# Feature-major rotary queries and key in an MLA layer, with the parts placed by DMAs

## The chip, the cores and the metric

One core of one Trainium2 chip runs the whole program. The metric is the device time of one execution in microseconds; the time of a kernel is the median of its runs. The engines are called by their short names: PE (TensorE, matmuls), ACT (ScalarE), DVE (VectorE), POOL (GpSimd) and SP (SyncE, which here only issues DMAs). A name such as SPq stands for the queue that an engine issues from.

## The reference

A trunk of two layers over 512 tokens of width 1024. Layer 0 is multi-head latent attention (MLA), layer 1 is gated linear attention (GLA); each is followed by a squared-ReLU MLP, and a final RMSNorm ends it. Only the MLA mixer is changed here:

```python
def mla_mixer(xn, positions, w_in, q_norm, w_uq, kv_norm, w_ukv, w_o):
    h = xn @ w_in                                  # 1024 -> 384 + 256 + 64
    c_q, c_kv, k_rope = h[..., :384], h[..., 384:640], h[..., 640:]
    q  = (rms_norm(c_q,  q_norm)  @ w_uq ).reshape(B, S, 8, 128 + 64)
    kv = (rms_norm(c_kv, kv_norm) @ w_ukv).reshape(B, S, 8, 128 + 128)
    q_nope, q_rope = q[..., :128], q[..., 128:]
    k_nope, v      = kv[..., :128], kv[..., 128:]
    cos, sin = rope_tables(positions)              # 32 frequencies
    q_rope = apply_rope(q_rope, cos, sin)          # (t1 cos - t2 sin, t2 cos + t1 sin)
    k_rope = apply_rope(k_rope, cos, sin)          # one rotary key for all heads
    # scores = (q_nope . k_nope + q_rope . k_rope) * 192**-0.5, causal softmax, times v, times w_o
```

All inputs and outputs are float32.

## The kernel before

Precision comes from splitting: a float32 operand becomes a rounded part `hi` and a rest `lo`, both in the matmul's fp32r format, and `mm3` multiplies them in three matmuls (L107 to L112). `split` makes `hi` on ACT and `lo` on DVE. Activations are kept feature-major, that is features in the 128 partitions and the 512 tokens along the free axis.

The order of instructions on each engine is made by a scheduler when the program is built: it goes by the order of the text and by its own estimate of when each operand is ready. Each engine then works its list strictly in order and waits on semaphores. `tc.issue_after` and `keep_in_program_order` put instructions behind others in that order. SP's queue is also such a list: a DMA that waits holds back those behind it. Tiles come from pools with a fixed number of buffers: raw weights (`wraw`) have two, the `hi` and `lo` weights (`wh`, `wl`) three each, scratch (`tmp`) six, and `slot("B")` sixteen. The accumulators (PSUM banks) have three tags: "a" with two banks, "b" and "c" with three each.

The MLA function goes through these steps:

- The latents: `pkv` (two banks, L402 to L409) and the three query latents `CQ`. `latent` (L382) makes their parts and sums their squares. Neither latent is normalised before it is used: the 1/rms of each token is applied later.
- The raw rotary key (L440 to L450): weights with `lo` in 64 columns and `hi` in 64, 16 matmuls, and a copy `kr` of all 128 rows.
- The means (L453 to L459): eight matmuls with stationary tiles 96 wide, three rows of 32 equal lines, for the latent keys, the queries and x. `rsqrt` (Ln and Exp on ACT, then three steps on DVE) turns them into `rows`.
- V (L462 to L513): 8 blocks of 6 matmuls. After the third block `rows` is turned into columns `cols` by four transposes, and `evac_v` copies V out, scaled by a column. Row 0 is split and spread over 128 partitions by two matmuls (L505) into `r_kv`, which scales the latent keys `CKV`.
- The rotary tables: `rope_turns` (L293) works out the angles in turns on POOL from `gains`, with tokens in the partitions and (4 tiles x 32 frequencies) along the free axis. `rope_tables` (L346) takes the Sin after the V blocks, between two table loads of ACT, and scales one copy of the tables for the queries and one by x's 1/rms for the key.
- The key is turned token-major by four transposes (L519), rotated, and turned back by four (L611); `KA` and `KB` hold its parts in opposite halves.
- The rotary queries (L528 to L543): 36 matmuls, token-major, four tiles. `rotate_q(t, g)` (L626) rotates a tile of four heads, part of it on POOL for the second group. `turn_q` (L637) turns two heads back by four transposes and makes their parts.
- `project(h)` (L547) makes the other 128 features of q and k; `scores`, `turn` and `values` are the attention proper, and project the heads two ahead.

At the start the loads go out on SP's queue and two of x on ACT's (L1397 to L1408), and `exp_set` loads ACT's table for Ln and Exp.

Of the kernel before, what the change touches and what calls it, by code (L numbers as in the profile page):

```python
# [18 lines left out]
P = 128  # L19
D = 1024  # L20
# [18 lines left out]
SCALE = (NOPE + ROPE) ** -0.5  # L39
# [9 lines left out]
def trunk_kernel(ctx: ExitStack, tc: tile.TileContext, t_in: dict, out: bass.AP, out_row: bass.AP):  # L49
# [98 lines left out]
    gains = const.tile([P, N_GAIN + NT + 32], F32, name="gains")  # L148
    pos_i = gains[:, N_GAIN : N_GAIN + NT].bitcast(I32)
    invf = gains[:, N_GAIN + NT :]  # L150
# [33 lines left out]
    row_eps = rk.tile([3 * RB, 1], F32, name="row_eps")  # L184
    DVE.memset(row_eps[: 2 * RB], EPS * EPS)
    DVE.memset(row_eps[2 * RB :], EPS)

    def row_weights(name, *parts):
        t = rk.tile([P, 3 * RB], F32, name=name)
        DVE.memset(t, 0.0)  # L190
        for lo, hi, v in parts:
            DVE.memset(t[:, lo * RB : hi * RB], v)
        both = tuple(rk.tile([P, 3 * RB], F32R, name=name + x) for x in "hl")
        split(t, *both, hi_eng=DVE)
        return both

    mean_kv = row_weights("mean_kv", (0, 1, 1.0 / KL))
    mean_q = row_weights("mean_q", (1, 2, 1.0 / QL))
    mean_x = row_weights("mean_x", (0, 2, EPS / D), (2, 3, 1.0 / D))

# [4 lines left out]
    def rsqrt(r, m, n, eps=eps_t):  # L205
# [9 lines left out]
        DVE.scalar_tensor_tensor(r, b, 1.5, y0, ALU.add, ALU.mult)  # L215
# [77 lines left out]
    def rope_turns():  # L293
        sh = (P, NT, 32)
# [3 lines left out]
        def tmp(shape, dt=F32):  # L298
            return rp.tile(list(shape), dt, tag="rope", bufs=8, name=uname("rope"))

        pos = tmp((P, NT))
        POOL.tensor_copy(pos, pos_i)
        ang, part = tmp(sh), tmp(sh)
        POOL.tensor_tensor(
            ang, pos.unsqueeze(2).to_broadcast([P, NT, 32]), invf.unsqueeze(1).to_broadcast([P, NT, 32]), ALU.mult
        )
# [30 lines left out]
        r = rk.tile([P, 2, NT, 32], F32, name="rope_turns")  # L337
        for n, shift in enumerate((0.25, 0.0)):
            t = tmp(sh)
            POOL.tensor_scalar(t, acc, 1.0, shift, ALU.mult, ALU.add)  # L340
            wrap(t)
            POOL.tensor_scalar(r[:, n], t, 0.4999999, -0.4999999, ALU.min, ALU.max)
# [3 lines left out]
    def rope_tables(r, rx):  # L346
        tabs = rk.tile([P, 2, NT, 32], F32, name="rope_tabs")
        tc.keep_in_program_order(ACT.activation(tabs, r, AF.Sin, scale=2.0 * float(np.pi)))
# [5 lines left out]
        return tabs[:, 0], tabs[:, 1], tabs_q[:, 0], tabs_q[:, 1]  # L354
# [19 lines left out]
    def mla(layer, nrm, first, pools):  # L374
# [7 lines left out]
        def latent(psum, g, hi, lo, acc):  # L382
            ACT.activation(hi, psum, AF.Copy, scale=g)
            DVE.scalar_tensor_tensor(lo, psum, g, f(hi), ALU.mult, ALU.subtract)
            if not acc:
                acc.append(f(slot("B")))
                ACT.activation(acc[0], psum, AF.Square)
            else:
                sq = tmp()
                ACT.activation(sq, psum, AF.Square)  # L390
                DVE.tensor_tensor(acc[0], acc[0], sq, ALU.add)
            return hi, lo
# [26 lines left out]
        for j in range(2):  # L419
# [3 lines left out]
            if j == 0:  # L423
                for i in range(2):
                    CVL.append(latent(pkv[i], gcol("kvn", 2 * layer + i), slot("B"), slot("B"), kv_sq))
# [24 lines left out]
        ACT.activation(kr, p, AF.Copy)  # L450


        means = bank("c")[: 3 * RB, :]  # L453
        mm3(means, mean_x, nrm.sums, True, False)
# [1121 lines left out]
```

## Time and profile before

| | us |
|---|---|
| median of 3 runs | 1088.0 (1087.83 to 1088.02) |
| the profiled execution | 1088.19 |
| its span | 1086.5 |

| engine | busy us | share of the span | instructions |
|---|---|---|---|
| PE | 1077.8 | 99% | 5376 |
| DVE | 861.3 | 79% | 1431 |
| ACT | 550.0 | 51% | 928 |
| POOL | 41.8 | 4% | 72 |

The profile comes from one execution. Times in a timeline count from the start of the span: first column the start, second the duration, then engine, line, operation, output and inputs, shape and count; in brackets the idle time before and what ended it. Matmuls overlap, so the distance between starts tells what one costs, not its duration. A row of a table by windows has the stretch, its length, then the busy time and count of PE, PE's weight loads, DVE, ACT and POOL, the granted clock, the DMA share and GB/s. A row of a group has busy time and mean ns of one, then the idle time before. The attention layer takes about the first 155 us of the span.

### The profile page before, as it was taken

To read this page: it belongs to the slowest core of one execution; us is meant where nothing else is said; L and a number is where in the kernel's file an instruction comes from. 1 tells how busy PE (TensorE), PEld (TensorE's weight loads), DVE (VectorE), ACT (ScalarE), POOL (GpSimd) and SP (SyncE) were. 2 spreads that over 40 slices of the span, in tenths; PEclk is the share of its full clock that TensorE was granted. 3 is DMA by queue.
4 is the path that set the end of the run, shared out by engine and by line. 5 is a ranking of instruction groups with operands and counts; after the bars stand their busy time and mean duration, and the time that the engine had idled before them with its cause. 6 is when DMAs were issued, how large, how long until landed. Compare 5 with 4: busy or idle time off the path is not lost.

```text
span 1086.5 us, 14047 instructions
## 1 busy us (share of the span) xinstructions
PE 1077.8 (99%) x5376; PEld 910.7 (84%) x5376; DVE 861.3 (79%) x1431; ACT 550.0 (51%) x928; POOL 41.8 (4%) x72
## 2 busy tenths in 40 slices
PE   9999999999999999999999999999999999999997
PEld 7788888888888888888788888888888888888886
DVE  7889968987887977977686685569788797897885
ACT  7767655553453454445345736546445444344354
POOL 7310002000000000000000000000000000000000
PEclk9999999999999999999999999999999999999999
DMA  7311233142332332222222222232233233223222
GB/s 225 78 49 40 78 96 98 41 154 78 117 117 78 111 122 78 83 95 95 87 78 78 78 78 66 67 131 67 98 113 121 78 97 124 90 80 123 70 97 78
DMA packets 86004, 101.35 MB, mean 93 GB/s; under 512 B 7377, under 2 KB 63953, under 8 KB 85937
## 3 DMA queue, kind: packets, MB, share of 16 engines
q1 hardware_dynamic: 84128, 99.40, 28.5%
q10 hardware_dynamic: 1808, 1.05, 0.3%
q8 instruction: 42, 0.69, 0.3%
q14 instruction: 26, 0.20, 0.1%
HBM read 98.35 MB, written 2.10 MB: 92 GB/s over the span
## 4 chain that ended last, share of the span: by engine, by line
PE 97%; DVE 1%; DMA 0%; ACT 0%; issue 0%; SPq 0%; DVEq 0%; ACTq 0%
PE ps L110 21%; PE ps L112 21%; PE ps L111 21%; PE ps L922 17%; PE ps L923 9%; PE ps L1200 2%; PE ps L127 1%; PE ps L409 1%; PE ps L870 1%; PE ps L1271 0%; PE ps L670 0%; PE ps L1250 0%; PE ps L666 0%; PE ps L669 0%; DMA gains<-in_gains_dram 0%; PE ps L668 0%
## 5 line engine op out<-in xcount | busy, mean ns | idle before, releaser
L110 PE MATMUL ps<-set,wh 128*128 128x512 f32 x760 | 296.9, 391 | 0.0
L111 PE MATMUL ps<-set,wh 128*128 128x512 f32 x760 | 296.5, 390 | 0.0
L112 PE MATMUL ps<-set,wl 128*128 128x512 f32 x760 | 296.3, 390 | 0.0
L102 ACT ACTIVATE wh<-wraw 128x1024 fp32r<-128x1024 f32 x139 | 147.0, 1061 | 241.2 <-PE ps L111 115.3
L105 DVE TENSOR_TENSOR wl<-wraw,wh 128x1024 fp32r<-128x1024 f32 x139 | 169.9, 1222 | 42.0 <-ACT wh L102 41.8
L112 PEld LDWEIGHTS ps<-set,wl 128*128 128x128 f32 x760 | 142.7, 188 | 30.2
L110 PEld LDWEIGHTS ps<-set,wh 128*128 128x128 f32 x760 | 142.7, 188 | 29.8
L111 PEld LDWEIGHTS ps<-set,wh 128*128 128x128 f32 x760 | 142.8, 188 | 27.5
L922 PE MATMUL ps<-T,wh 128*128 128x512 f32 x448 | 157.5, 391 | 0.0
L923 PE MATMUL ps<-T,wl 128*128 128x256 f32 x448 | 126.2, 282 | 0.0
L922 PE MATMUL ps<-set,wh 128*128 128x512 f32 x336 | 119.9, 397 | 0.0
L922 PEld LDWEIGHTS ps<-T,wh 128*128 128x128 f32 x448 | 84.1, 188 | 18.2
L923 PE MATMUL ps<-set,wl 128*128 128x256 f32 x336 | 94.2, 280 | 0.0
L105 DVE TENSOR_TENSOR wl<-comb,wh 128x1024 fp32r<-128x1024 f32 x42 | 51.3, 1222 | 47.1 <-ACT wh L102 47.1
L836 DVE TENSOR_TENSOR xT<-ps,xT 128x512 f32<-128x512 f32 x120 | 82.2, 685 | 6.7 <-PE ps L112 6.7
L102 ACT ACTIVATE wh<-comb 128x1024 fp32r<-128x1024 f32 x42 | 44.6, 1061 | 83.3 <-PE ps L922 81.8
L923 PEld LDWEIGHTS ps<-T,wl 128*128 128x128 f32 x448 | 84.6, 189 | 0.5
L922 PEld LDWEIGHTS ps<-set,wh 128*128 128x128 f32 x336 | 63.1, 188 | 15.1
L940 DVE TENSOR_TENSOR tmp<-ps,tmp 128x512 f32<-128x512 f32 x98 | 67.2, 685 | 0.9
L923 PEld LDWEIGHTS ps<-set,wl 128*128 128x128 f32 x336 | 63.4, 189 | 1.6
L110 PE MATMUL ps<-wh,set 128*128 128x512 f32 x144 | 58.8, 409 | 0.0
L102 ACT ACTIVATE wh<-raw 128x1024 fp32r<-128x1024 f32 x28 | 29.5, 1054 | 56.7 <-PE ps L922 55.8
(381 smaller groups left out, 1666.1 us busy)
## 6 DMA issues: line engine op xcount, KB each, us to landing
wraw<-in_mlp_w_up_dram SPq DMA_DIRECT2D x32, 1024.0 KB, 5.3
wraw<-in_mlp_w_down_dram SPq DMA_DIRECT2D x18, 1024.0 KB, 5.1
raw<-in_mlp_w_down_dram SPq DMA_DIRECT2D x14, 1024.0 KB, 5.0
wraw<-in_gla_w_in_dram SPq DMA_DIRECT2D x12, 1024.0 KB, 5.2
wraw<-in_mla_w_o_dram SPq DMA_DIRECT2D x4, 1024.0 KB, 5.2
wraw<-in_gla_w_o_dram SPq DMA_DIRECT2D x4, 1024.0 KB, 5.3
xT<-in_x_dram SPq DMA_DIRECT2D x6, 256.0 KB, 5.4
wraw<-in_mla_w_in_dram SPq DMA_DIRECT2D x3, 512.0 KB, 7.1
```

The source lines that it names most:

```text
L102: order(ACT.activation(hi, src, AF.Copy))
L105: lo_eng.tensor_tensor(lo, src, f(hi), ALU.subtract)
L110: PE.matmul(psum, wh, xh, start=start, stop=False)
L111: PE.matmul(psum, wh, xl, start=False, stop=False)
L112: PE.matmul(psum, wl, xh, start=False, stop=stop)
L127: PE.transpose(psum, src, ident[: src.shape[0], : src.shape[0]])
L409: PE.matmul(p, w[:, i, j * P : (j + 1) * P], x, start=start, stop=stop)
L836: DVE.tensor_tensor(xT[m], p, xT[m], ALU.add)
L922: PE.matmul(o.rearrange("p (h t) -> p h t", h=2), wh, x, start=start and k == 0, stop=False, skip_group_check=True)
L923: PE.matmul(o[:, :TH], wl, x[:, 0], start=False, stop=k == KH - 1, skip_group_check=True)
L940: DVE.tensor_tensor(by_tile(r), high, by_tile(r), ALU.add)
L1200: PE.matmul(p[:, t - t0], k[:, t * P : (t + 1) * P], moving[:, t], start=True, stop=True)
```

## The change

Rotary queries and key stay feature-major. The tables have the 32 frequencies in rows, four times over, and the tokens along the free axis. The host lays the rotary columns of `w_uq` out as a new input `w_qr`, in the order group of four heads, half, head, frequency, and the positions as a new input `pos`, spread over partitions; `pos` is loaded on ACT's queue.

- `rope_turns` works with (4 tiles x 32 frequencies) in partitions and 128 tokens free; its last step writes four 32-row pieces to the first 32 rows of a [128, 2, 512] tile, twice. `rope_tables` copies these 32 rows to the other three quarters by six DMAs on SP, issued after the load of V's weights; then a Sin of 1024 elements in a row, issued after the first half of the rotary projection is copied out. ACT starts with the table set for Sin, and the set for Ln and Exp is loaded after the Sin only.
- The rotary projection is done in two groups, with weights stationary and the latents moving, ahead of the means and of V. `rotate_q(g)` rotates four heads in six DVE operations of 512 elements, makes two `hi` (ACT) and two `lo` (DVE) with the scale of the scores, and 16 DMAs on SP place the 32-row parts, four for each head, in that head's tile `QST`. The transposes of `turn_q` go.
- The key: the two halves are added from the bank, rows are scaled by x's 1/rms (now rows 64 to 127 of `rows`), the halves are swapped by two ACT copies, and three DVE operations rotate. Its eight transposes go.
- The means: six matmuls 128 wide, none split. x's mean goes to a bank of its own and is scaled by a column (`row_mix`) on DVE and added. A factor of 0.75 in the queries' mean makes its weight a power of two; `SCALE` makes up for it.
- The spread of the latent keys' 1/rms row by two matmuls becomes four DMAs on SP of 32 rows each. The rows are turned to columns after the second block of V instead of the third.
- `CVL` and the first group's raw queries have tiles of their own instead of `slot("B")`.
- `rotate_q(1)` stands at head 1 of the attention loop. The load of the second `wraw_qn` is issued behind the first group's DMAs, and the splits of the first projections behind the third evacuation of V.

```diff
+Q_PART = 0.75
+SCALE = (Q_PART / (NOPE + ROPE)) ** 0.5
...
+    row_eps = rk.tile([P, 1], F32, name="row_eps")
+    row_mix = rk.tile([P, 1], F32, name="row_mix")
...
+    mean_kv = row_weights("mean_kv", 0, 1.0 / KL)
+    mean_q = row_weights("mean_q", 1, Q_PART / QL)
...
+            for i in range(NT):
+                POOL.tensor_scalar(
+                    r[:32, n, i * P : (i + 1) * P], t[i * 32 : (i + 1) * 32], 0.4999999, -0.4999999, ALU.min, ALU.max
+                )
...
+    def rope_tables(r, behind, evacuated):
+        for n in range(2):
+            for i in range(1, 4):
+                with tc.issue_after(behind.ins):
+                    SP.dma_start(r[i * 32 : (i + 1) * 32, n], r[:32, n])
+        with tc.issue_after(evacuated.ins):
+            tc.keep_in_program_order(ACT.activation(r, r, AF.Sin, scale=2.0 * float(np.pi)))
         exp_set()
-        tabs_q = rk.tile([P, 2, NT, 32], F32, name="rope_tabs_q")
-        DVE.tensor_scalar(tabs_q, tabs, SCALE, None, ALU.mult)
-        DVE.tensor_tensor(tabs, tabs, rx.unsqueeze(1).unsqueeze(3).to_broadcast([P, 2, NT, 32]), ALU.mult)
+        return r[:, 0], r[:, 1]
...
+        def project_rope(g):
+            for a in range(2):
+                p = bank("b")
+                for k in range(3):
+                    c = (2 * g + a) * P
+                    mm3(p, cut(wq[k], slice(None), slice(c, c + P)), CQ[k], k == 0, k == 2)
+                QR[g, a] = room(g, f"qr{a}")
+                evacuated = ACT.activation(QR[g, a], p, AF.Copy)
+            return evacuated
+
+        cos, sin = rope_tables(turns, loaded, project_rope(0))
+        mean_x, mean_l = bank("c"), bank("c")
+        for i in range(2):
+            PE.matmul(mean_x, inv_dr, nrm.sums[i], start=i == 0, stop=i == 1)
+        for i in range(2):
+            PE.matmul(mean_l, mean_kv, kv_sums[i], start=i == 0, stop=False)
+        for i in range(2):
+            PE.matmul(mean_l, mean_q, q_sums[i], start=False, stop=i == 1)
+        part = tmp()
+        DVE.tensor_scalar(part, mean_x, row_mix, None, ALU.mult)
+        means = tmp()
+        DVE.tensor_tensor(means, mean_l, part, ALU.add)
+        rows = sb.tile([P, S], F32, tag="rstd", bufs=2, name=uname("rstd"))
+        rsqrt(rows, means, S, row_eps)
+        project_rope(1)
...
+        def rotate_q(g):
+            u, v = QR[g, 0], QR[g, 1]
+            ys = []
+            for a, (c, d, op) in enumerate(((cos, sin, ALU.subtract), (sin, cos, ALU.add))):
+                y, t = tmp(), tmp()
+                DVE.tensor_tensor(y, u, c, ALU.mult)
+                DVE.tensor_tensor(t, v, d, ALU.mult)
+                DVE.tensor_tensor(y, y, t, op)
+                ys.append(y)
+            parts = []
+            for y in ys:
+                hi = slot("B")
+                ACT.activation(hi, y, AF.Copy, scale=SCALE)
+                parts.append(hi)
+            for y, hi in zip(ys, parts[:2]):
+                lo = slot("B")
+                DVE.scalar_tensor_tensor(lo, y, SCALE, f(hi), ALU.mult, ALU.subtract)
+                parts.append(lo)
+            for h in range(HH):
+                q = QST[g * HH + h] = slot("B")
+                for i, part in enumerate(parts):
+                    moved[g] = SP.dma_start(f(q[i * H : (i + 1) * H]), f(part[h * H : (h + 1) * H]))
+
+        rotate_q(0)
...
-                if (t, hf) == (1, 0):
+                if (t, hf) == (0, 1):
                     pr = bank("b")
...
-            if t == 1:
-                wide = bank("c")
-                parts = tuple(sb.tile([1, S], F32R, tag="tmp", bufs=6, name=uname("tmp")) for _ in range(2))
-                split(rows[0:1], *parts)
-                for i in range(2):
-                    PE.matmul(wide, ones_r[0:1], parts[i], start=i == 0, stop=i == 1)
+            if t == 0:
                 r_kv = sb.tile([P, S], F32, tag="rstd", bufs=2, name=uname("rstd"))
-                ACT.activation(r_kv, wide, AF.Copy)
+                for i in range(P // RB):
+                    SP.dma_start(r_kv[i * RB : (i + 1) * RB], rows[:RB])
...
+        DVE.tensor_tensor(kr[k_rows], kr[k_rows], rows[k_rows], ALU.mult)
+        ka, kb = tmp(), tmp()
+        lead, trail = slice(ROPE, ROPE + H), slice(ROPE + H, P)
+        ACT.activation(kb[lead], kr[trail], AF.Copy, scale=-1.0)
+        ACT.activation(kb[trail], kr[lead], AF.Copy)
+        DVE.tensor_tensor(ka[k_rows], kr[k_rows], cos[k_rows], ALU.mult)
+        DVE.tensor_tensor(kb[k_rows], kb[k_rows], sin[k_rows], ALU.mult)
+        DVE.tensor_tensor(ka[k_rows], ka[k_rows], kb[k_rows], ALU.add)
...
-        started = []
+        started = [evacuated[2].ins]
...
+            if h == 1:
+                rotate_q(1)
...
+    ACT.dma_start(pos_i, t_in["pos"])
...
-    exp_set()
+    tc.keep_in_program_order(ACT.preload_act_table_set("trig_and_small"))
```

More of the change, by code (lines that the diff above doesn't have):

```diff
@@ L647, in mla @@
-        for t in range(NT):
-            rotate_q(t, 0)
-        turn_q(0)
+            return tc.issue_after(started[-1])
+        proj = {0: project(0)}
+        proj[1] = project(1, "b")
         pre.close()
@@ L739, in mla @@
         probs = scores(0, *proj[0])
-        turn_q(2)
         for h in range(MH):
```

203 lines of the change are left out of this document (64 added, 139 removed).

## The prediction

> **What bounds the kernel now.** I read the page first, then the chain of waits, then the timelines of the engines from 30 to 95 us, where the edited code runs, and last the groups of VectorE instructions there.
>
> ```profile
> span 1086.5 us, 14047 instructions
> PE 1077.8 (99%) x5376; PEld 910.7 (84%) x5376; DVE 861.3 (79%) x1431; ACT 550.0 (51%) x928; POOL 41.8 (4%) x72
> PE 97%; DVE 1%; DMA 0%; ACT 0%; issue 0%; SPq 0%; DVEq 0%; ACTq 0%
> ...
> 44.00:52.00 8.00, 8.00 (x37) 6.16 (x38) 6.92 (x12) 6.80 (x12) 0.00 (x0) 1.00 0.08 23
> 52.00:60.00 8.00, 8.00 (x38) 6.63 (x37) 7.24 (x18) 6.53 (x9) 0.00 (x0) 1.00 0.35 98
> 60.00:68.00 8.00, 8.00 (x38) 6.42 (x38) 6.07 (x15) 4.47 (x10) 2.25 (x3) 1.00 0.00 1
> ```
>
> TensorE (PE) is busy 99% of the span, and the chain of what ended last lies on it for 97%. In the edited stage it is busy for the whole of each 8 us window (the column after the length), while VectorE (DVE) is busy 6.9, 7.2 and 6.1 us and ScalarE (ACT) 6.8, 6.5 and 4.5. So there are two questions: how much PE time the change takes out, and whether DVE, ACT or a transfer becomes late enough to give PE a wait that it does not have now. The profiled execution took 1088.19 us, 1.69 us more than its span, and lies 0.19 us above the median of 1088.0; I work against 1088.19 and take the 0.19 off at the end. About 0.2%, 2.2 us, is what a measurement of this kernel can tell from no change.
>
> **What leaves PE.** Because busy PE time overlaps, I price instructions by the distance between starts.
>
> ```profile
> 33.66 0.39 PE L447 MATMUL ps<-set,w_kr 128*128 128x512 f32 x1
> ...
> 37.29 0.40 PE L110 MATMUL ps<-set,mean_xh 128*96 128x512 f32 x1
> ...
> 40.06 0.39 PE L110 MATMUL ps<-wh,set 128*128 128x512 f32 x1
> ...
> 45.29 0.39 PE L112 MATMUL ps<-wh,set 128*128 128x512 f32 x1
> ...
> 46.60 0.39 PE L111 MATMUL ps<-wl,set 128*128 128x512 f32 x1
> ...
> 51.82 0.60 PE L127 MATMUL ps<-ident,kr 128*128 128x128 f32 x4
> ...
> 52.49 0.40 PE L111 MATMUL ps<-wl,cq0h 128*128 128x512 f32 x1
> ...
> 63.99 0.60 PE L127 MATMUL ps<-ident,tmp 128*64 128x128 f32 x4
> ...
> 64.66 0.39 PE L111 MATMUL ps<-cq0l,wh 128*128 128x512 f32 x1
> ...
> 67.91 0.60 PE L127 MATMUL ps<-ident,set 128*128 128x128 f32 x4
> 68.34 0.39 PE L663 MATMUL ps<-kf,qf 128*128 128x128 f32 x2
> ...
> 68.92 0.60 PE L127 MATMUL ps<-ident,set 128*128 128x128 f32 x4
> ...
> 69.65 0.50 PE L666 MATMUL ps<-kh,qh 128*128 128x512 f32 x1
> ...
> 92.69 1.03 PE L127 MATMUL ps<-ident,set 128*128 128x128 f32 x8
> 93.94 0.49 PE L663 MATMUL ps<-kf,qf 128*128 128x128 f32 x2 [0.22 <-ACT pr L121]
> ```
>
> The 16 matmuls of the rotary key fill 33.66 to 37.29, so one 512-column matmul costs 3.63/16 = 0.227 us. Then, one by one:
> - Means: from 37.29 to 40.06 stand the eight 96-wide matmuls and three of V. 2.77 - 3 x 0.227 = 2.09 us; six of 0.227 make 1.36. Gain 0.73.
> - The broadcast of the key's 1/rms row (two matmuls of L505 and their switches): 45.29 to 46.60 holds them and two of V, 1.31 - 0.45 = 0.86. Gain 0.86.
> - Turning the raw key (51.82): four transposes and one matmul until 52.49, 0.67 - 0.23 = 0.44. Turning the rotated key back (63.99 to 64.66): 0.44 again.
> - `turn_q`, four calls of four transposes: 0.43 at 67.91; 0.73 - 0.23 = 0.50 at 68.92; and two calls together from 92.69 to 93.94, 1.25, of which 0.22 is a wait that may stay, so 1.03. Together 1.96.
>
> The sum is 4.4 us. The 36 matmuls of the rotary projection stay, with operands exchanged and 512 columns each; the four small transposes of the 1/rms rows stay too (64 wide instead of 96), at no change.
>
> **What DVE and ACT gain or lose.**
>
> ```profile
> L645 DVE TENSOR_TENSOR set<-ps,set 64x512 fp32r<-64x512 f32 x8 | 5.5, 688 | 0.2
> L478 DVE SCALAR_TENSOR_TENSOR set<-ps,cols,set 128x512 fp32r<-128x512 f32 x6 | 4.2, 744 | 0.2 <-ACT set L477 0.2
> L594 DVE TENSOR_TENSOR tmp<-set,rope_tabs_q 128x256 f32<-128x256 f32 x8 | 3.3, 415 | 0.6 <-ACT set L543 0.5
> L596 DVE TENSOR_TENSOR set<-tmp,tmp 128x128 f32<-128x128 f32 x8 | 2.7, 334 | 0.0
> L597 DVE TENSOR_TENSOR set<-tmp,tmp 128x128 f32<-128x128 f32 x8 | 2.2, 281 | 0.0
> L595 DVE TENSOR_TENSOR tmp<-set,rope_tabs_q 128x256 f32<-128x256 f32 x4 | 1.7, 416 | 0.0
> L391 DVE TENSOR_TENSOR set<-set,tmp 128x512 f32<-128x512 f32 x1 | 0.7, 693 | 0.7 <-ACT tmp L390 0.7
> ```
>
> The old rotation and turning of queries costs DVE 5.5 + 3.3 + 2.7 + 2.2 + 1.7 = 15.4 us. The new `rotate_q` has six tensor_tensor of 512 (0.69, row L391) and two scalar_tensor_tensor (0.74, row L478): 5.6 us a group, 11.2 for both. The key's chain and the means come out about even, so DVE has some 3 to 4 us less in all. But the first group, 5.6 us, now stands with the rsqrt of the rows, six evacuations of V (4.2 us), the latent keys and the key's rotation between the Sin and the first scores. ACT loses eight half copies of `turn_q` and one table load, and gains a Sin four times as long and the copies of the parts.
>
> **The chain that decides: POOL, table DMAs, Sin, rows.**
>
> ```profile
> 32.74 1.15 POOL L342 TENSOR_SCALAR rope_turns<-rope 128x128 f32<-128x128 f32 x1
> 36.45 0.29 POOL L342 TENSOR_SCALAR rope_turns<-rope 128x128 f32<-128x128 f32 x1
> 36.07 1.49 SPq L551 DMA_DIRECT2D wraw_qn<-in_mla_w_uq_dram  x3
> 40.26 0.69 ACT L121 ACTIVATE tmp<-ps,row_eps 96x512 f32<-96x512 f32 x1
> 43.14 0.69 DVE L215 SCALAR_TENSOR_TENSOR rstd<-tmp,tmp 96x512 f32<-96x512 f32 x1
> 53.14 1.28 ACT L348 ACT_TABLE_LOAD   x1
> 54.44 0.42 ACT L348 ACTIVATE rope_tabs<-rope_turns 128x256 f32<-128x256 f32 x1
> L102 ACT ACTIVATE wh<-wraw 128x1024 fp32r<-128x1024 f32 x139 | 147.0, 1061 | 241.2 <-PE ps L111 115.3
> tmp<-in_gla_w_in_dram ACTq DMA_DIRECT2D x1, 64.0 KB, 2.3
> ```
>
> Today the turns are ready at 36.45 + 0.29 = 36.74 and wait 17.7 us for the Sin at 54.44; the 1/rms rows are done at 43.14 + 0.69 = 43.83, before any Sin. Afterwards the Ln and Exp of the rows stand behind `exp_set`, that behind the Sin, and the Sin behind six DMAs and the POOL chain. That is the added wait; behind it on ACT queue the rows, the hi parts of the queries and V's evacuations, and V's banks wait for these.
>
> The end of POOL: two clamps become eight, and the two rows above bound one between 0.29 and 1.15. Six more at their mean of 0.72 are 4.3 us: 41.0 (38.5 to 43.6). SP issues three DMAs in 1.49, 0.50 each; a 32-partition one may be cheaper, and nothing here shows one. The last of the second table's three goes out at 42.0 and lands 2.3 us later by the 64 KB row, at 44.3. A 1024-element Sin is taken at the 1.06 of an ACTIVATE of that length: 45.4. Table load: 46.7. Ln to the last rsqrt step took 43.83 - 40.26 = 3.57: rows at 50.2 (47.7 to 52.8 with POOL's ends).
>
> PE meanwhile: after 37.29 it has 18 matmuls of the first rotary half (41.4), six means (42.7), the second half (46.8) and two blocks of V, 12 matmuls (49.55). If the turning of the rows into columns stands there, PE waits 0.7 us (0 to 3.3). If it is queued behind further V blocks, three of them fit in the banks, 4.1 us, and the wait is nothing. I take 0.7.
>
> **Three smaller terms.**
> - The start: positions are one more load on ACT's queue, among loads that are just in time:
>
> ```profile
> 10.28 1.41 ACT L249 ACTIVATE set<-xT,gains 128x512 fp32r<-128x512 f32 x2 [0.38 <-DMA xT<-in_x_dram]
> ```
>
> One issue of 0.50 that pushes the later x tiles costs 0 to 0.5; I take 0.2. (Below nothing is excluded: no load is taken out of that order.)
> - The split of the first `wraw_qn`: three wh buffers are held by the rotary piece and both pieces of V. V used to be followed by the 36 rotary matmuls, now `project(0)` comes directly. The buffer comes free when the first piece of V is done, three matmuls (0.68) before V's end, and then
>
> ```profile
> 56.66 0.84 ACT L102 ACTIVATE wh<-wraw_qn 128x768 fp32r<-128x768 f32 x1
> 57.55 0.95 DVE L105 TENSOR_TENSOR wl<-wraw_qn,wh 128x768 fp32r<-128x768 f32 x1
> ```
>
> must run. hi is there 0.84 - 0.68 = 0.16 us late, lo at 1.11, two matmuls (0.45) after q's start: 0.7 at most, and 0 if the k half (six matmuls, 1.36) goes first. I take 0.4.
> - The first scores: V ends at 49.55 + 36 x 0.227 + 0.5 = 58.2, two projections of 15 matmuls bring PE to 65.0. From 45.4 DVE has 19.6 us for 2.1 (rsqrt), 5.6 (rotation), 4.2 (V), 2.9 (latent keys), 4.1 (key), 2.2 (two splits: 0.95 below, and a third more elements, 1.2) and 2.5 (projections' evacuations, at the 0.69 of row L391 or less) = 23.6, so it can be up to 4 us behind. `project(2)`, 3.4 us, can run meanwhile: 0 to 4, I take 0.5, nearer the low end as PE has that filler.
>
> Other additions cost nothing while this cover holds: the four DMAs of the key's 1/rms (rows 50.2 + three issues 1.5 + 2.3 = 54.0, latent keys 2.9 later at 56.9, needed at 58.2 plus q's nine matmuls, 60.2) have 3.3 us to spare; the first head's four DMAs are out by about 56 and landed by 58.3 against 65.0; the second group has until the scores of head 4.
>
> Net: -4.4 + 0.7 + 0.2 + 0.4 + 0.5 = -2.6. 1088.19 - 2.6 = 1085.6, on the scale of the median 1085.4 us; its own range, with waits from 0.8 to 3, is 1084.4 to 1086.6.
>
> **Rivals.**
> - A, everything is covered: the 4.4 us come whole, 1083.6. For it: PE is busy 8.00 of 8 us in each window quoted, without a gap, and DVE and ACT get less work. Against it: the chain above has lost its 17.7 us of slack.
> - B, the tables come late and DVE piles up, and the gain is eaten: every clamp at the 1.15 end gives rows at 52.8 and a wait of 3.3, so -4.4 + 3.3 + 1.1 = 0.0, 1088.0. For it: POOL's like instructions already spread fourfold, 0.29 and 1.15. The Trainium skill ("SBUF — State Buffer", Who interferes with whom) says that a VectorE instruction with two SBUF inputs locks out a GpSimd one that reads SBUF; by that rule the upper end is the likelier beside a busy VectorE, and the spread of the two rows agrees. Against it: V's spare banks.
> - C, slower: the order on SP's queue. `rotate_q(0)` stands in the text ahead of the four DMAs that spread the key's 1/rms. If its 16 DMAs are queued first, they start when the parts are made, 45.4 + 5.6 + 2.1 + a hi copy = about 53.7, and take 16 x 0.50 = 8.0; the four follow, the last issued at 63.2 and landed at 65.5; the latent keys are ready 2.9 later at 68.4, while PE, with both q halves pulled ahead, needs them at 62.3. That wait of 6.1 and the 1.3 before it give +3.0: 1091.0. It decides once over three of the parts go ahead. For it: SP works in order, and 42 DMAs are new on it. Against it: the rows are ready (50.2) before the parts.
>
> **Chances and range.** The forecast 0.40, A 0.20, B 0.22, C 0.18. Faster by over 0.2% are A and four fifths of the forecast: 0.52. Within: the last fifth and B, 0.30. Slower: 0.18. The range 1083.4 to 1091.0 reaches from A to C and leaves some 0.15 out.
>
> **What would show it.** In the new profile: no transposes of `kr`, `tmp` or `set` on PE, six 0.227 us means; POOL's end at 38.5 to 43.6 and the Sin near 44; a PE wait on the rows' transposes of under 1 us; `rstd` DMAs out before the queries' parts; DVE without gaps from 45 to 65. PE waits in sum over 2.2 us between 37 and 70, or new ones in the attention loop, would make it wrong.

## The result, and the profile after

The changed kernel takes 1089.93 us (median of 22 runs, 1087.44 to 1091.48), the kernel before 1087.76 us (22 runs on the same chips, 1087.29 to 1088.55). The ratio is 1.0017, 95% interval 1.0012 to 1.0023: slower by some 2 us, inside the range on record, but on the other side of zero from the forecast. In the groups of experiments below the kernel before ran again, at medians of 1087.64 to 1087.80.

The profiled execution took 1089.9 us with a span of 1088.2. First the windows of the three stretches that the change touches, kernel before: up to the means, from there to the first scores, and the attention loop. The columns are length, busy time of PE, weight loads, DVE, ACT and POOL, granted PE clock, DMA share, GB/s.

```profile
0.00:37.29 37.29, 35.80 (x155) 30.02 (x156) 30.41 (x57) 26.08 (x40) 30.23 (x54) 1.00 0.63 185
37.29:68.34 31.05, 30.93 (x142) 24.14 (x140) 25.60 (x50) 22.24 (x38) 2.25 (x3) 1.00 0.24 68
68.34:131.88 63.54, 63.12 (x363) 53.95 (x362) 60.45 (x182) 44.31 (x117) 0.77 (x1) 1.00 0.16 50
```

The same stretches of the changed kernel (the second now starts with the first rotary matmul, as the means stand behind it):

```profile
0.00:36.80 36.80, 35.62 (x155) 30.05 (x155) 29.06 (x55) 26.09 (x40) 29.80 (x52) 1.00 0.62 189
36.80:73.58 36.78, 30.81 (x125) 23.57 (x124) 27.47 (x42) 22.19 (x36) 5.04 (x9) 0.95 0.41 104
73.58:133.60 60.02, 60.02 (x348) 52.49 (x347) 56.76 (x171) 42.11 (x113) 0.00 (x0) 1.00 0.27 80
```

The attention loop became 3.52 us shorter. The start won 0.49, but in the profiles of the changed kernel's variants below (without experiment 5) it took 36.49 to 38.44, so this may be chance. The middle stage became 5.73 us longer, although PE has 17 recorded instructions fewer to do in it: PE is now idle for 6 of its 36.78 us, and part of the rest ran at a lower clock. The waits of PE in the first 160 us, with their total, count and longest, name where:

```profile
PE ps L129 <- DVE rstd L216: 2.6, 1, 2.6
PE ps L112 <- ACT wh L104: 2.6, 1, 2.6
PE ps L1401 <- DVE ones L169: 1.2, 1, 1.2
PE ps L112 <- ACT set L104: 0.8, 1, 0.8
```

The third stands at the start and was there before. The first is the wait on the 1/rms rows, the second that on the split of the first `wraw_qn`, the fourth a new one in the rotary projection. The rows' chain in the timeline, in the order in which it hands on (start, duration, engine, in brackets the idle time before):

```profile
5.54 0.58 POOL L303 CAST rope<-pos_i 128x128 f32<-128x128 int32 x1 [3.93 <-DMA pos_i<-in_pos_dram]
39.63 2.79 POOL L343 TENSOR_SCALAR rope_turns<-rope 32x128 f32<-32x128 f32 x4
37.95 6.27 SPq L354 DMA_DIRECT2D rope_turns<-rope_turns  x6
46.24 1.06 ACT L356 ACTIVATE rope_turns<-rope_turns 128x1024 f32<-128x1024 f32 x1 [3.36 <-DMA rope_turns<-rope_turns]
48.61 0.72 ACT L123 ACTIVATE tmp<-tmp,row_eps 128x512 f32<-128x512 f32 x1
50.37 0.75 DVE L213 SCALAR_TENSOR_TENSOR tmp<-tmp,row_eps,tmp 128x512 f32<-128x512 f32 x1 [6.01 <-ACT tmp L123]
51.76 0.68 DVE L515 TENSOR_TENSOR tmp<-qr,rope_turns 128x512 f32<-128x512 f32 x1
52.37 0.69 DVE L216 SCALAR_TENSOR_TENSOR rstd<-tmp,tmp 128x512 f32<-128x512 f32 x1
53.20 0.43 PE L129 MATMUL ps<-ident,rstd 64*128 64x64 f32 x4 [2.58 <-DVE rstd L216]
```

POOL ends at 42.42, the Sin starts at 46.24 after 3.36 us of waiting for the table DMAs, and the rows are done at 53.06. An instruction of the query rotation (L515) was put between two steps of the rows on DVE, as the tables were there first. What happened on PE right after that wait:

```profile
54.38 0.63 PE L112 MATMUL ps<-wh,cv1h 128*128 128x512 f32 x1
54.81 0.63 PE L113 MATMUL ps<-wl,cv1h 128*128 128x512 f32 x1
...
57.78 0.40 PE L114 MATMUL ps<-wh,cv1l 128*128 128x512 f32 x1
```

From 54.38 on eight equal matmuls start 0.427 us apart; the same matmuls behind them, from 57.78 to 63.37, start 0.233 us apart. The granted clock is 0.50 from 54.34 to 57.75, 3.41 us, and 1.00 before and behind. That costs 8 x 0.19 = 1.5 us and no wait shows it. The second big wait, with ACT's order ahead of it:

```profile
62.75 0.69 ACT L542 ACTIVATE set<-ps,cols 128x512 f32<-128x512 f32 x1
63.45 0.63 ACT L584 ACTIVATE tmp<-kr 32x512 f32<-32x512 f32 x1
64.09 0.69 ACT L542 ACTIVATE set<-ps,cols 128x512 f32<-128x512 f32 x1
64.79 0.63 ACT L585 ACTIVATE tmp<-kr 32x512 f32<-32x512 f32 x1
65.44 1.58 ACT L104 ACTIVATE wh<-wraw_qn 128x768 fp32r<-128x768 f32 x2
66.34 0.50 PE L112 MATMUL ps<-cq0h,wh 128*128 128x512 f32 x1 [2.57 <-ACT wh L104]
```

V's last matmul starts at 63.37. The split could have followed then, but two copies of the key's halves (L584, L585) and the last two evacuations of V stand ahead of it on ACT.

The sum by the distance between starts, each less the 0.233 of a matmul: 0.98 (first wait) + 2.75 (rows) + 1.5 (half clock) + 2.74 (split) = 8.0 us lost in the middle stage. The stage became only 5.7 longer, so 2.3 us of PE work were saved in it; this figure is a difference and not measured by itself. The loop won 3.5 and the start 0.5. 8.0 - 6.3 = +1.7, the difference of the two profiled executions, 1089.9 and 1088.19. As the 2.3 is a difference, the sum says that nothing changed behind the loop, and no more.

### The profile page after: what moved, and what is told of

It is laid out like the page before. It is cut to its first block, busy times and chain, and to the rows that moved or that the text cites. A ratio compares the mean times of both kernels' runs of the same rounds, so it can differ in the third digit from the quotient of the medians.

```text
span 1088.2 us, 14042 instructions
## 1 busy us (share of the span) xinstructions
PE 1074.5 (99%) x5348; PEld 908.9 (84%) x5348; DVE 857.2 (79%) x1406; ACT 547.8 (50%) x923; POOL 43.4 (4%) x74
## 4 chain that ended last, share of the span: by engine, by line
PE 94%; DMA 2%; DVE 1%; ACT 1%; issue 1%; SPq 0%; DVEq 0%; ACTq 0%
PE ps L112 20%; PE ps L114 20%; PE ps L113 20%; PE ps L910 17%; PE ps L911 9%; PE ps L1188 2%; PE ps L129 1%; PE ps L858 1%; DMA xT<-in_x_dram 1%; DMA wraw<-in_mla_w_in_dram 1%; DMA wraw_v<-in_mla_w_ukv_dram 1%; PE ps L1259 0%; PE ps L664 0%; PE ps L663 0%; PE ps L660 0%
## 5 line engine op out<-in xcount | busy, mean ns | idle before, releaser
L112 PE MATMUL ps<-wh,set 128*128 128x512 f32 x128 | 52.5, 410 | 0.0
```

The costliest lines, as they stand in the source:

```text
L112: PE.matmul(psum, wh, xh, start=start, stop=False)
```

## The experiments

All are edits of the changed kernel, each timed beside the kernel before (ratios are to that kernel; a bracket behind a ratio is its 95% interval). "Changed" below is its 1089.93 us.

**1. The rows ahead of the Sin.** The start preloads the Exp table again, and the Sin, its table load and the reload behind it are called after `rsqrt`:

```diff
-    tc.keep_in_program_order(ACT.preload_act_table_set("trig_and_small"))
+    exp_set()
...
-        cos, sin = rope_tables(turns, loaded, project_rope(0))
+        copied = project_rope(0)
...
         rsqrt(rows, means, S, row_eps)
+        cos, sin = rope_tables(turns, loaded, copied)
```

> Edit: ScalarE computes the 1/rms rows (Ln, Exp) first and the Sin of the tables after them, at the price of one more load of function tables (1.28 us) ahead of the Sin. Own theory: the 2.6 us wait of TensorE on the rows in the changed kernel is the chain POOL, table DMAs, Sin, load, Ln. With the rows ahead of the Sin they are ready at about 48, before TensorE asks for them at 50.4; the wait and the half clock that followed it (1.6 us) go, the query rotation starts some 2 us later. Changed kernel 1089.9 - 2.6 - 1.6 = 1085.7 us; mean granted clock 0.998 to 0.999. Rival (VectorE and ScalarE are simply full between the Sin and the first scores, the wait only moves): a wait of 2 to 4 us appears before the first scores, 1088 to 1090 us.

Measured: 1086.78 us (11 runs, 1085.22 to 1087.92), 0.9989 (0.9980 to 0.9998), 3.15 us below changed. The rows and the columns in the timeline:

```profile
48.81 1.06 ACT L356 ACTIVATE rope_turns<-rope_turns 128x1024 f32<-128x1024 f32 x1
49.05 0.69 DVE L216 SCALAR_TENSOR_TENSOR rstd<-tmp,tmp 128x512 f32<-128x512 f32 x1
52.26 0.46 PE L129 MATMUL ps<-ident,rstd 64*128 64x64 f32 x4
```

The rows are ready at 49.74, 2.5 us before PE turns them (1.6 of these because this profile is late already at the first rotary matmul, 38.44 for 36.80); there is no wait and no half clock after it, and no new wait behind the Sin, which is 2.6 us later. The rival is out: the wait did not move. That it missed my 1085.7 by 1.1 us has no shown cause; the wait on the split stays, at 2.1. The order of one Sin and one Ln, not the amount of work, made this part of the loss: the edit even adds a table load.

**2. The rows turned into columns two V blocks later.**

```diff
-                if (t, hf) == (0, 1):
+                if (t, hf) == (1, 1):
...
-                    for i in ((0, 0, first_v), (0, 1, p)):
+                    for i in (*first_v, (1, 1, p)):
```

> Edit: TensorE turns the rows into columns after the fourth block of V instead of the second; the V blocks stay in their banks until then, nothing else changes. Own theory (the wait is a matter of where the transposes are queued): rows at 53.1 against TensorE at 50.4 + 2.7 for two more blocks = 53.1, so the wait of 2.6 us falls under 0.5, and the half clock (1.6 us) has no gap to follow; the evacuations of four blocks then come in a heap, and TensorE may wait 0 to 1.2 us for a bank. 1089.9 - 2.1 - 1.6 + 0.6 = 1086.8 us. Rival (the evacuations on ScalarE and VectorE are what the rest waits for, and these start no earlier): the wait comes back at the split of wraw_qn or at the first scores, 1088.9 us or more.

Measured: 1091.93 us (5 runs, 1091.56 to 1092.49), 1.0040: slower still, a miss for my theory by 5 us. The wait on the rows is gone, but a new one stands three matmuls later, on a VectorE copy of 0.16 us:

```profile
56.41 0.69 DVE L526 SCALAR_TENSOR_TENSOR set<-tmp,set 128x512 fp32r<-128x512 f32 x1
57.01 0.16 DVE L563 COPY cols<-ps 128x8 f32<-128x8 f32 x1
57.22 0.59 PE L112 MATMUL ps<-wh,cv0h 128*128 128x512 f32 x1 [2.17 <-DVE cols L563]
```

With the transposes later, the copy that makes the columns is queued on DVE behind the query rotation (six instructions of `rotate_q` and the scaling of the key run between the rows at 52.6 and this copy at 57.01). No block of V can be evacuated before it, so PE runs out of banks. Both remaining waits (2.3 and 3.2 us by starts) were followed by half clock, and all five runs have a mean clock of 0.996. Turning the rows later is no cover: what the rows release has to come early.

**3. The key's rotation behind project(0) in the text.** The block from `DVE.tensor_tensor(kr[k_rows], ...)` to the two subtractions that make KA and KB is moved as it is:

```diff
-        DVE.tensor_tensor(kr[k_rows], kr[k_rows], rows[k_rows], ALU.mult)
-        ...
         proj = {0: project(0)}
+        DVE.tensor_tensor(kr[k_rows], kr[k_rows], rows[k_rows], ALU.mult)
+        ...
```

> Edit: the text of the key's rotation (kb copies on ScalarE, the four products and the splits on VectorE) stands behind project(0) instead of ahead of it, so the split of the first wraw_qn is queued on ScalarE ahead of the two kb copies. Own theory: the 2.57 us wait of TensorE on that split is mostly ScalarE's order (two kb copies of 0.64 and the last evacuations of V ahead of it), the buffer itself is free at about 63.5; the wait falls to 0.5 to 1.2. 1089.9 - 1.4 to - 2.1 = 1087.8 to 1088.5 us. Rival (the wait is for the wh buffer, as the prediction had it): 2.5 us stays, 1089.9. A second rival: the key comes later, and the first scores wait for it what was won, 1089.9, with a new PE wait at 72 to 74.

Measured: 1089.75 us (11 runs, 1087.85 to 1091.22), 1.0016: no change against changed. The profiled execution is one of the short ones, 1088.79, without half clock. ACT now makes the first half of the split at 61.57, ahead of both kb copies, and PE's waits of that stage are:

```profile
PE ps L129 <- DVE rstd L216: 1.8, 1, 1.8
...
PE ps L112 <- ACT wh L104: 0.8, 1, 0.8
PE ps L114 <- DVE wl L107: 0.7, 1, 0.7
PE ps L658 <- ACT pr L123: 0.7, 1, 0.7
```

The split's wait fell from 2.6 to 0.8, as the order on ACT would have it and the buffer would not. What was won came back: 0.7 for the low half of k's weights on DVE, 0.2 for KB at the first scores (71) and 0.7 for a head's probabilities in the loop (95), each some 0.2 more by starts. That is the second rival, spread out. ACT's order is shown as the cause of the wait; the move alone is not shown to be worth anything.

**4. PE kept busy while it waits for the rows.**

```diff
                 if (t, hf) == (0, 1):
+                    idle = bank("c")
+                    for _ in range(11):
+                        PE.matmul(idle, inv_dr, CVL[0][0], start=True, stop=True)
```

> Edit: eleven additional 512-column matmuls into a spare bank (their result is not read) stand ahead of the transposes of the rows, so that TensorE is busy (11 x 0.227 = 2.5 us) where it waited 2.6 us; the rows come no earlier. Own theory (the eight V matmuls of 0.427 us after the wait are a half-rate clock that follows the idle gap): no stretch of half clock after 53, mean clock 0.998 to 0.999, 1089.9 - 1.6 = 1088.3 us. Rival (the eight were slowed by the traffic of the query DMAs and VectorE, not by a gap): they still take 0.427 us each and the time stays 1089.9.

Measured: 1089.77 us (11 runs, 1087.88 to 1091.43), 1.0018: the time did not fall by the expected 1.6. The windows say what became of it:

```profile
50.00:60.00 10.00, 10.00 (x47) 7.86 (x46) 9.92 (x17) 5.07 (x9) 0.00 (x0) 1.00 0.27 65
```
```profile
61.98:65.39 3.41, 1.59 (x8) 0.97 (x7) 3.37 (x6) 3.37 (x6) 0.00 (x0) 1.00 0.42 99
65.39:68.81 3.42, 3.42 (x10) 2.64 (x9) 3.29 (x5) 1.67 (x3) 0.00 (x0) 0.50 0.61 162
```

Without the gap there is no half clock between 50 and 60, with the same DMAs (0.27 of the engines' time, 0.28 in the changed kernel) and a DVE as busy (9.92 and 9.53 us), which rules these out as its cause. But in this execution the half clock followed the second gap (2.0 us by starts) instead. So the mechanism holds and its worth was wrong: taking away one gap helps little as long as another can halve the clock. That is not the whole of the miss, though: five of the 11 runs have a mean clock of 0.999, so no half clock in this stage (one such stretch of 3.41 us takes 0.0016 off the mean), and of these two took 1087.88 and 1088.12 but three 1089.22 to 1089.84. What held those three is open.

**5. The eight clamps on VectorE instead of GpSimd.**

```diff
-                POOL.tensor_scalar(
+                DVE.tensor_scalar(
                     r[:32, n, i * P : (i + 1) * P], t[i * 32 : (i + 1) * 32], 0.4999999, -0.4999999, ALU.min, ALU.max
```

> Edit: the eight clamps of the table chain run on VectorE instead of GpSimd; the order Sin, then rows, stays as in the changed kernel. It tests whether GpSimd's end (42.4 us) sets the Sin (46.2) and so the rows (53.1). Own theory: yes, it does; the clamps are ready some 2 to 4 us earlier, the Sin and the rows come as much earlier, the 2.6 us wait of TensorE falls below 1 and no half clock follows there: 1089.9 - 2 to - 4 = 1086 to 1088 us. Rival (the Sin is late for another reason: the six DMAs on SyncE, or ScalarE's own order): the Sin stays within 0.7 us of 46.2 and the time at 1089.9. A price in both: eight more instructions on VectorE before 40, where it is about 79% busy.

Measured: 1098.58 us (5 runs, 1097.61 to 1103.13), 1.0107. It did not answer its question. VectorE in the timeline:

```profile
27.27 0.92 DVE L343 TENSOR_SCALAR rope_turns<-rope 32x128 f32<-32x128 f32 x4 [9.77 <-POOL rope L324]
28.22 1.51 DVE L107 TENSOR_TENSOR wl<-wraw,wh 128x1024 fp32r<-128x1024 f32 x1
```

A clamp on DVE waits 9.77 us for POOL's angles, and a weight split stands behind it; PE waits 9.0 us for that. Neither theory had priced this wait, although the question that the prediction asks of ACT (what is queued behind the instruction that waits) would have shown it. Experiment 9 puts the question again.

**6. The rows ahead of the Sin, and q split ahead of k in project(0).** Beside the edit of experiment 1:

```diff
                 raw = sb.tile([P, 2, 4, NOPE], F32, tag="wraw", bufs=2, name=uname("wraw_kn"))
...
-                with afterwards():
-                    wk["p"] = piece(raw.rearrange("p k h c -> p k (h c)"), 2, 512)
+                wk["raw"] = raw
             if h % 2 == 0:
                 ...
                     wn["p"] = piece(raw, 3, 256)
+            if h % 4 == 0:
+                with afterwards():
+                    wk["p"] = piece(wk["raw"].rearrange("p k h c -> p k (h c)"), 2, 512)
```

> Edit: the rows ahead of the Sin (as in the first experiment), and the first wraw_qn is split ahead of the first wraw_kn, so that it takes the buffer of the first rotary piece, free at 49.2, and the k piece takes the one that V's first weights hold until about 61. Own theory (of the remaining 2.1 us wait at 61 about 1.5 is ScalarE's order, 0.5 the buffer): the wait on the q piece is gone; the k piece's split now comes 1 to 2 us after V's end, but nine to ten q matmuls (2.1 us) can run before it: waits of 0 to 1 in sum, 1086.8 - 1.1 to - 2.1 = 1084.7 to 1085.7 us. Rival (VectorE, without a gap from 47 to 75, holds it): the wait moves to the k piece or to the first scores, 1086.5 to 1087.5.

Measured: 1086.02 us (11 runs, 1085.24 to 1087.45), 0.9983 (0.9974 to 0.9991). The wait after V fell from 2.1 in experiment 1 to 1.1 and 0.4, now for the k piece and the low half of it. The time is 0.8 us below experiment 1, between the two expectations; the intervals of the two overlap, so the waits show the effect better than the time.

**7. The rows ahead of the Sin, and the key's rotation on GpSimd.**

```diff
-        DVE.tensor_tensor(kr[k_rows], kr[k_rows], rows[k_rows], ALU.mult)
+        POOL.tensor_tensor(kr[k_rows], kr[k_rows], rows[k_rows], ALU.mult)
...
-        ACT.activation(kb[trail], kr[lead], AF.Copy)
+        POOL.tensor_copy(kb[trail], kr[lead])
```

> Edit: the rows ahead of the Sin, and the key's rotation (scaling by the rows, two shifted copies, two products, one sum: on ScalarE 1.25 us, on VectorE 2.75 us) runs on GpSimd, which is idle after 42. Own theory (ScalarE's and VectorE's order delays the split of the first wraw_qn): hi is made at about 61.2 instead of 62.5, the 2.1 us wait falls to 0.8 or less, the key is ready in time (due 70.5): 1086.8 - 1.3 to - 2 = 1084.8 to 1085.5 us. Rival (GpSimd beside VectorE slows both, and its six instructions of 512 elements take over 2 us each): the first scores wait for KA, and 1087 to 1089.

Measured: 1089.05 us (11 runs, 1088.43 to 1089.97), 1.0014: 2.3 us worse than experiment 1. Not for the rival's reason: POOL took 0.6 to 1.8 us for each, and the key was ready at 59.66, early. (One multiplication of DVE that ran beside POOL's first took 1.82 us instead of 0.69, so one did slow the other there.) ACT:

```profile
60.96 0.63 ACT L593 ACTIVATE KA<-tmp 64x512 fp32r<-64x512 f32 x1
61.61 0.63 ACT L594 ACTIVATE KB<-tmp 64x512 fp32r<-64x512 f32 x1
62.27 0.69 ACT L543 ACTIVATE set<-ps,cols 128x512 f32<-128x512 f32 x1
62.85 1.57 ACT L104 ACTIVATE wh<-wraw_qn 128x768 fp32r<-128x768 f32 x2
```

As the key is early, its two copies into KA and KB, due only at the first scores, take exactly the places that the kb copies left, ahead of the split. PE waits 3.7 us, and half clock follows. It is the same mechanism as in the changed kernel, by other instructions.

**8. The turning transposes put back.**

```diff
+        def turn_again():
+            p = bank("c")
+            for t in range(NT):
+                tr(p[:, t * P : (t + 1) * P], f(KA)[:, t * P : (t + 1) * P])
```

called once before and once behind the first scores and twice at head 2.

> Edit: the changed kernel with sixteen additional 128x128 transposes of the key's tile at the four places where the queries were turned before (into a spare bank, not read); it tests what their removal was worth. Theory 1, the prediction's price: 16 transposes of 0.12 us = 1.96 us: 1089.9 + 2.0 = 1091.9 us. Theory 2 (the transposes also cost their neighbours: each switch between the two kinds of matmul input, and the wait for a free bank; the attention stage gained 3.5 us where 1.5 was priced): +3 to +3.5, 1093 us. Theory 3 (TensorE has slack there, as VectorE is busy 56.8 of 60.0 us in that stage): under +1.

Measured: 1090.57 us (5 runs, 1090.54 to 1093.14), 1.0034. By the time alone, 0.6 above changed, the third theory would hold. But the time says little, since in this profile the rows' wait was 0.6 and not 2.6. The stage says more: from the first scores to the last matmul of the last head, in the kernel before, the changed one, and this one:

```profile
68.34:148.70 80.36, 79.94 (x458) 68.51 (x457) 72.99 (x223) 53.54 (x143) 0.77 (x1) 1.00 0.15 47
```
```profile
73.58:150.57 76.99, 76.99 (x445) 67.21 (x443) 68.51 (x211) 51.33 (x139) 0.00 (x0) 1.00 0.21 63
```
```profile
72.86:151.22 78.36, 78.36 (x457) 68.78 (x456) 67.96 (x209) 50.95 (x139) 0.00 (x0) 1.00 0.21 61
```

The twelve transposes in this stretch cost 78.36 - 76.99 = 1.37 us, as priced (12 x 0.12); without them the stretch also took 76.91 and 76.93 us in experiments 1 and 9. So PE has no slack there. The other 2.0 us of 3.4 come from elsewhere in the loop: 0.4 us of PE idle time, and distances of up to 0.37 us (0.50 once) behind single matmuls, that the changed kernel no longer has. DVE has 4.5 us less there. Which part of the change does it was not tried.

**9. A shorter GpSimd chain.**

```diff
             POOL.tensor_scalar(t, acc, 1.0, shift, ALU.mult, ALU.add)
-            wrap(t)
```

> Edit: the changed kernel without the last reduction of the angles to one turn ahead of the clamps (six GpSimd instructions, 3.7 us; the tables are then not those of the reference); nothing else is moved. It tests the link from GpSimd's end to the rows, which moving the clamps to VectorE could not, as that blocked VectorE. Own theory: GpSimd ends at about 38.7 instead of 42.4, the Sin starts at about 43 instead of 46.2, the rows come about 3 us earlier; the 2.6 us wait falls below 0.5 and no half clock can follow it: 1089.9 - 2.1 to - 3.7 = 1086.2 to 1087.8 us. Rival (TensorE's means or ScalarE's copies of the rotary halves hold the rows, not the tables): wait and time as in the changed kernel, 1089 to 1091 us.

Measured: 1086.25 us (11 runs, 1085.35 to 1088.33), 0.9987 (0.9979 to 0.9996). POOL, ACT and DVE in the timeline:

```profile
32.70 4.50 POOL L342 TENSOR_SCALAR rope_turns<-rope 32x128 f32<-32x128 f32 x8
43.39 1.06 ACT L355 ACTIVATE rope_turns<-rope_turns 128x1024 f32<-128x1024 f32 x1
49.52 0.69 DVE L216 SCALAR_TENSOR_TENSOR rstd<-tmp,tmp 128x512 f32<-128x512 f32 x1
```

POOL ends at 37.20, the Sin follows its ACT neighbours without a wait, the rows are done at 50.21, and PE's wait on them is gone. That is the link which experiment 5 could not test: in the changed kernel, POOL and the table DMAs set the rows. With the rows at 50.2, where the prediction had put them, the kernel takes 1086.25, 0.85 above its forecast.

**10. Experiment 6, and the last third of `wraw_qr` split earlier.**

```diff
-        q_sums = parts_of(q_sq[0], lambda: slot("B"))
...
         wq = [cut(wa, slice(None), 0), cut(wa, slice(None), 1), wb]
+        q_sums = parts_of(q_sq[0], lambda: slot("B"))
```

> Edit: as the sixth experiment (rows ahead of the Sin, wraw_qn split ahead of wraw_kn), and the split of the last third of wraw_qr stands in the text ahead of the splitting of the query's sums of squares. Own theory (the first wait of TensorE, about 1 us at 39, is ScalarE's order: the copy of that third stands behind the sums' split, which waits 1.5 us for VectorE): the third is made at about 33, the wait is gone, 1086.0 - 1.0 = 1085.0 us. Rival (ScalarE and VectorE hold the later stages anyhow, and TensorE waits 1 us longer before the first scores): 1086.0.

Measured: 1085.01 us (11 runs, 1084.42 to 1088.59), 0.9979 (0.9971 to 0.9988), what my theory said, though its interval too overlaps with that of experiment 6. The copy of that third, at 38.74 in the changed kernel behind a split that waits 1.49 us for DVE, now stands at

```profile
31.99 0.63 ACT L104 ACTIVATE set<-wraw_qr 128x512 fp32r<-128x512 f32 x1 [1.25 <-DMA wraw_qr<-in_w_qr_dram]
```

and the wait near 39 is gone. Faster than both kernels, by 4.9 us than the changed one and 2.8 than the one before. That it comes to within 0.4 us of the forecast's 1085.4 is in part luck: waits of 1.8 us remain ahead of the first scores, and the loop gives 80.36 - 77.38 = 2.98 us where 1.5 was priced. One of the waits looks like the price of the later Sin: PE waits 0.4 us (0.9 in experiment 11) at the transposes, 50.50, although the rows are done at 47.49. By the order of the banks they need the one of a rotary half whose copy on ACT, from 49.80, stands behind the Sin and both table loads; no run tested this.

**11. Experiment 10, and the key's rotation behind project(0).** The edits of 10 and 3 together.

> Edit: as the tenth, and the key's rotation stands in the text behind project(0). Own theory: the two kb copies no longer stand ahead of the splits of wraw_kn and of the second wraw_qn on ScalarE, and the waits of 1.1 and 0.4 us after V fall below 0.5 in sum: 1085.0 - 1.0 = 1084.0 us. Rival (as in the third experiment: the key comes later, and the first scores and the next project wait instead, 0.4 + 0.9): 1085 to 1086 us.

Measured: 1085.28 us (11 runs, 1084.84 to 1088.92), 0.9979 (0.9970 to 0.9988): the same as 10. The first scores come at 66.53 instead of 68.45, and the stretch from there to the last head's last matmul takes 79.06 instead of 77.38 us. As the rival said, 1.7 of 1.9 us are given back in the loop. PE is idle there for 0.9 us (79.06 - 78.20) instead of 0.25; the rest of the 1.7 has no named cause.

## Why the prediction was wrong, step by step

- **PE work removed, 4.4 us: nearly right.** The twelve transposes in the loop are worth 1.37 (1.47 priced); the middle stage has 2.3 less by difference, where 2.96 was priced.
- **The rows' chain: the right mechanism, the term mis-sized. This is the first step that failed.** "I take 0.7" was 2.6 (2.75 by starts). Of the 2.9 us by which the rows were late (53.06 against 50.2), POOL's end gives 1.4: it started 0.65 later (5.54 against 4.89), because it waits for the positions, and the rest was slower; each clamp at 2.79/4 = 0.70 was right. The last three table DMAs are issued from 42.42 to 44.22, in 1.80 us where 1.49 was taken, and the Sin starts 1.9 later than forecast (46.24 for 44.3): 0.5 more. Two instructions stand between the rows' steps, a copy of a rotary half on ACT (0.5) and L515 on DVE (0.6), which makes the rows' steps 0.9 longer than the 3.57 taken. PE came to the rows 0.9 late itself, by the first wait, which is why the wait is 2.6 and not 3.5. Experiments 1 and 9, from two sides, give 3.2 and 3.7 us for having the rows on time, the half clock behind the wait included.
- **The half clock was not in the sum.** It added 1.5 us to a wait. The alternative that I offered, the transposes behind further V blocks with a wait of nothing, was wrong as well: experiment 2 shows that it makes things worse, as the columns' copy falls behind the query rotation on DVE.
- **The split of the first `wraw_qn`: "0.7 at most", measured 2.7. This is the second step that failed, and here the mechanism was wrong.** I costed the buffer alone (about 0.5 us of it) and not ACT's order, in which the key's copies, moved there by the change, stand ahead of the split. Experiments 3, 6 and 7 show the order by moving it each way.
- **A wait that I did not see: 0.98 us in the rotary projection.** The projection now comes directly after the key's projection, while the last third of its weights was still split late. Experiment 10 removes it.
- **First scores, 0.5: too high**, there is no wait at them. **The start, +0.2: not shown.** First matmuls stood at 5.24 to 5.78 in the changed kernel and its variants and at 5.70 before.
- **The loop: 3.5 us where 1.5 was priced**; 2.0 of it without a named cause.
- **The rivals.** B, 0.0, came nearest to the measured +1.7, and it was right in part: the tables came late. It had the rows at 52.8 by slower clamps, though; they came at 53.06 with clamps at the mean that I took, so that its nearness is partly luck. Its other half, DVE piling up, is not what PE waited for. C did not occur: the rows' four DMAs went ahead of the queries' sixteen.

```profile
53.08 3.35 SPq L572 DMA_DIRECT2D rstd<-rstd  x4
56.53 10.52 SPq L531 DMA_DIRECT2D set<-set  x16
```

With -2.6 forecast, the misses add up to 0.7 (work in the middle stage) + 2.0 (rows) + 1.5 (clock) + 2.3 (split) + 1.0 (first wait) - 0.5 (scores) - 0.7 (start) - 2.0 (loop) = +4.3, and -2.6 + 4.3 is the +1.7 of the profiles (the first of these is the difference named above). The forecast's own test, waits of over 2.2 us in sum between 37 and 70, came out against it: 6.0.

## What to carry to other kernels

When a change moves work off a saturated engine, write the in-order queue of every helper engine as it will be after the change, and ask for each moved instruction what will stand behind it: here a Sin ahead of a Ln, and two small copies ahead of a split, cost more than all the TensorE work that was taken out. Two orders of the same instructions (and one table load) differed by 3 us (experiment 1) and, with two more orders put right, by 5 (experiment 10). In this kernel a wait of 2 us or more on TensorE could cost half as much again in clock, depending on where it fell, and with one of two such waits gone the other could still do so, so mend them together.

## What the runs showed of the hardware

- **A gap far below 3.4 us can halve the clock; where it falls decides.** In the profiles of the changed kernel and its variants (without experiment 5), gaps (by starts) of 3.1, 3.2 and 3.9 us were each followed by a stretch of half clock; of 2.0 to 2.75 us some were (2.34, 1.99, and the first 2.75 of the changed kernel) and some not (2.27, 2.00, 2.73, and the second, 2.74, of the changed kernel); of 0.6 to 1.8 us none. The half clock began between 0.2 us before the gap's end and 1.1 us after it, and lasted 3.41 us. The Trainium skill ("TensorE: Matmul & The Clock Gate", Part 1) gives a free-running window of 3413 ns, which the trace agrees with; its table ("Why this matters for your kernels") warns of gaps over about 3 us, and here 2.0 to 2.75 were enough in some cases.

The traces also say which. The granted clock changes in steps of 3.413 us: in the changed kernel it is full from 6.55 us, half from 54.34 (14 steps later) and full from 57.75 (one more); in experiment 9 it is full from 7.31, so each profile has its own grid. Cut on their grids, the 13 profiles have some 4100 windows of 3.413 us. All 17 windows in which PE is idle for 1.82 us or more, by the profile's busy time, were followed by half clock, and none of the others, the longest idle time of which is 1.79. The two nearest are the window of experiment 4 shown there (busy 1.59 of 3.41, then 0.50) and this one of experiment 9, whose gap of 2.73 lies in two windows:

```profile
58.51:61.92 3.41, 1.63 (x7) 0.96 (x6) 3.35 (x6) 3.35 (x7) 0.00 (x0) 1.00 0.47 112
61.92:65.34 3.42, 2.65 (x11) 2.05 (x12) 3.31 (x6) 1.47 (x3) 0.00 (x0) 1.00 0.42 99
```

As an estimate from these figures, with the grid anywhere: a gap of 2.58 us idle, such as either of the two of the changed kernel, leaves 1.8 us in one window in about 0.7 of all cases.

- **The half clock goes with most of the spread, and with the size of the loss.** Of the 22 runs of the changed kernel the three with a mean clock of 0.999 took 1087.44 to 1087.85 us, as long as the kernel before; the seven with 0.996 took 1090.02 to 1091.48.
- **A 64 KB DMA of 32 partitions was no cheaper to issue than a load of 128.** In the changed kernel each of the six of the tables took SyncE 0.51 to 0.60 us, each part of the first `wraw_qn` 0.51 to 0.53; from issue to landing the six took 2.0 us (median).
